# Two transformer blocks on one core: the last output product as a stage of its own, with the roots of its norms on ScalarE and VectorE

## The chip, the cores and the metric

The kernel runs on one core of one Trainium2 chip. The metric is the device time of one execution in microseconds (us), as the median of the runs shown.

## What is computed

The input x has 512 positions of 1024 values in fp32. It goes through two blocks, each applied for two layers. The first block mixes by retention, two convolutions and a gated feed-forward part. The second block mixes by a gated spatial product, by attention and by a linear recurrence. Both end with the same pattern: a merged activation is multiplied by an output matrix, the result is normalised by its root mean square and scaled by a gain, and x is added. The change touches the last time this happens, in the last layer of the second block:

```python
def rmsnorm_2(x, g):
    xf = x.astype(jnp.float32)
    y = xf * lax.rsqrt(jnp.mean(xf * xf, axis=-1, keepdims=True) + EPS)
    return (y * g.astype(jnp.float32)).astype(x.dtype)

def second_block(...):
    for l in range(L):
        ...
        merged = (jax.nn.sigmoid(g_a) * (y_a @ w_proj_a[l])
                  + jax.nn.sigmoid(g_b) * (y_b @ w_proj_b[l])
                  + jax.nn.sigmoid(g_c) * (y_c @ w_proj_c[l]))
        x = x + rmsnorm_2(merged @ w_out[l], post_norm_g[l])
    return x
```

## The kernel before, in words

The program is one long list of instructions, written in the order in which each engine is to run them; nothing reorders it afterwards. Every fp32 product is made as three products of split operands (`mm3`, lines 348 to 350): high times high, high times low, low times high, accumulated in one PSUM bank. Weights come in chunks of 128x1024 through a ring: SyncE (SP) loads them, ScalarE (ACT) makes the high part (line 208), VectorE (DVE) the low part (line 209).

`out_proj` makes the product of a merged activation with an output matrix. The 512 positions are four blocks of 128 rows (`tb`), the 1024 output columns two halves (`hf`), so there are eight PSUM banks in use. The first chunks of the contraction are run through all four blocks; the last four (`tail`) are run block by block, so that one half of one block after the other is finished. With `last=True`, which only the last layer of the second block passes, nothing but the end of the program follows.

What follows each half is the norm. `post_half` takes the sum of squares of a half on ScalarE (line 472, which writes the scaled sum into a column of the small tile `sq`; in the trace it is an ACTIVATE and a read of the accumulator) and multiplies the half by the gain on VectorE (line 478). After the second half VectorE adds the two sums and epsilon (line 476), and GpSimd (POOL) raises the result to the power -0.5 (line 402, `rstd`). `post_norm` then multiplies each half by that root and adds x (line 489, VectorE, two instructions). In the last product the two halves are written to the output straight away (line 564), the first by ScalarE's DMA queue, the second by SP's.

GpSimd has little else to do near the end: its last instructions before these four powers are the two DMA issues that fetch the gain (line 321).

Behind the last instruction of each engine stands the end of the program, which the profile gives to line 1625: each engine has a DRAIN and then takes part in a barrier of all five. SP first waits for all transfers to land. GpSimd collects the arrivals of the others behind its own DRAIN and releases them, clears the semaphores, and a second, like barrier follows.

Of the kernel before, what the change touches and what calls it, by code (L numbers as in the profile page):

```python
# [10 lines left out]
AF = mybir.ActivationFunctionType  # L11
ALU = mybir.AluOpType
# [6 lines left out]
NT = S // 128  # L19
EPS = 1e-6  # L20
# [126 lines left out]
class Stream:  # L147
# [102 lines left out]
    def next(self):  # L250
        return len(self.order) // UNITS
# [9 lines left out]
class Kernel:  # L261
# [202 lines left out]
    def post_half(self, tb, hf, ps, g):  # L464
# [15 lines left out]
        ys.append(y)  # L480
        return r

    def post_norm(self, tb, ps, g):

        r = self.post_half(tb, 1, ps, g)
        _, ys = self.post.pop(tb)
        for hf in range(2):
            x = self.x[tb, hf]
            self.nc.vector.scalar_tensor_tensor(x[:], ys[hf][:], r[:, 0:1], x[:], op0=ALU.mult, op1=ALU.add)
            self.s.f(ys[hf])  # L490

    def out_proj(self, name, l, nk, get, done, g_post, g_pre, spill, last=False, head=4, tail=4):


        ws = self.ws
        gp = [self.bcast(g_post, 512 * hf) for hf in range(2)]
        gn = None if last else [self.bcast(g_pre, 512 * hf) for hf in range(2)]
        ps = {}
        wts = {}

        def w(k):
            if k not in wts:
                wts[k] = [self.ws.take(512, (name, l, 128 * k, (512 * hf, 512))) for hf in range(2)]
            return wts[k]

        def go(k, tb, hfs=(0, 1)):
            op = get(k)
            for hf in hfs:
                if (tb, hf) not in ps:
                    ps[tb, hf] = self.p.t()  # L510
                wh, wl = w(k)[hf]
                t = slice(128 * tb, 128 * tb + 128)
                self.mm3(ps[tb, hf][:], (op.hi[:, t], op.lo[:, t]), (wh, wl), k == 0, k == nk - 1)

        base = ws.floor = ws.next()
        assert head + tail <= nk
        for k in range(head):
            for tb in (0, 1):
                go(k, tb)
            self.tick()  # L520
        for k in range(head):
            for tb in (2, 3):
                go(k, tb)
            done(k)
            ws.floor += 1
            self.tick()
        for k in range(head, nk - tail):
            for tb in range(NT):
                go(k, tb)
            done(k)  # L530
            ws.floor += 1
            self.tick()
        assert ws.floor == base + nk - tail
        for tb in range(NT):
            units = [(k, hf) for hf in range(2) for k in range(nk - tail, nk)]
            if tb == NT - 1 and not last:
                units.sort()
            nk_half = max(n for n, u in enumerate(units) if u[1] == 0)
            pre = ()
            for n, (k, hf) in enumerate(units):  # L540
                go(k, tb, (hf,))
                if n == 1 and not last:
                    if tb >= 2:
                        self.transposes(tb - 2)
                    if tb >= 1:
                        pre = self.pre_norm_parts(tb - 1, gn, spill)
                        next(pre)
                if n == nk_half:
                    if tb == NT - 1:
                        for _ in pre:  # L550
                            pass
                    self.post_half(tb, 0, ps[tb, 0], gp)
                    for _ in pre:
                        pass
                if tb == NT - 1 and hf:
                    done(k)
                    ws.floor += 1
                    if n < 4:
                        ws.ahead(base + nk + AHEAD - 2 + n // 2)
            self.post_norm(tb, ps[tb, 1], gp)  # L560
            if last:
                for hf in range(2):
                    eng = self.nc.sync if hf else self.nc.scalar
                    eng.dma_start(self.out[128 * tb:128 * tb + 128, 512 * hf:512 * hf + 512], self.x[tb, hf][:])
                    self.s.f(self.x.pop((tb, hf)))
        ws.floor = None
        self.s.f(*gp)
        if not last:
            self.pend = self.norm_tail(gn, spill)

    def norm_tail(self, gn, spill):

# [1056 lines left out]
```

## Time and profile before

| what | value |
|---|---|
| median of 3 runs | 3151.83 us (3151.82 to 3152.45) |
| the profiled execution, its own time | 3152.43 us |
| its span in the profile | 3150.7 us |
| granted TensorE clock, mean of the span | 0.999 of full speed |
| PE busy | 3135.4 us (100% of the span) |
| DVE, ACT, POOL busy | 1864.8, 1195.4 and 236.3 us |

The span is what the profiler sees from the first to the last instruction; the execution's own time is 1.73 us longer. The profiled execution is 0.60 us above the median of the runs, and at the upper end of their range. Busy times say which engine has work all the time; what the end of the program waits for is read from the last ten microseconds alone, where PE is already done.

### The profile page before, as it was taken

To read this page: it belongs to the slowest core of one execution; us is meant where nothing else is said; L and a number is where in the kernel's file an instruction comes from. 1 tells how busy PE (TensorE), PEld (TensorE's weight loads), DVE (VectorE), ACT (ScalarE), POOL (GpSimd) and SP (SyncE) were. 2 spreads that over 40 slices of the span, in tenths; PEclk is the share of its full clock that TensorE was granted. 3 is DMA by queue.
4 is the path that set the end of the run, shared out by engine and by line. 5 is a ranking of instruction groups with operands and counts; after the bars stand their busy time and mean duration, and the time that the engine had idled before them with its cause. 6 is when DMAs were issued, how large, how long until landed. Compare 5 with 4: busy or idle time off the path is not lost.

```text
span 3150.7 us, 36918 instructions
## 1 busy us (share of the span) xinstructions
PE 3135.4 (100%) x14814; PEld 2638.9 (84%) x14814; DVE 1864.8 (59%) x2731; ACT 1195.4 (38%) x1801; POOL 236.3 (8%) x365
## 2 busy tenths in 40 slices
PE   9999999999999999999999999999999999999998
PEld 7888888888888888888898888888889888888887
DVE  6687556663568755666458736745546854663643
ACT  4222343343422234333345626622325643642222
POOL 2000010000300010000011001200002000120000
PEclk9999999999999999999999999999999999999999
DMA  6222322232422232223323123332333313433232
GB/s 206 92 90 94 134 86 102 94 120 107 148 107 87 94 134 88 93 101 107 112 95 127 55 99 118 116 140 72 125 124 120 94 67 107 133 114 107 95 106 74
DMA packets 62336, 337.47 MB, mean 107 GB/s; under 512 B 10290, under 2 KB 10418, under 8 KB 27476
## 3 DMA queue, kind: packets, MB, share of 16 engines
q1 hardware_dynamic: 49840, 302.02, 27.4%
q0 software_dynamic: 11312, 31.45, 3.5%
q8 instruction: 117, 1.92, 0.3%
q10 hardware_dynamic: 1012, 1.64, 0.1%
q14 instruction: 55, 0.45, 0.0%
HBM read 310.16 MB, written 8.39 MB: 101 GB/s over the span
## 4 chain that ended last, share of the span: by engine, by line
PE 99%; DMA 0%; ACT 0%; DVE 0%; DVEq 0%; ACTq 0%; issue 0%; POOLq 0%
PE p L348 31%; PE p L350 31%; PE p L349 31%; PE p L452 1%; PE p L691 1%; PE p L1090 1%; PE p L1357 0%; PE p L1063 0%; PE p L1062 0%; PE p L1064 0%; PE p L1061 0%; PE p L1065 0%; DMA s<-in_x_dram 0%; PE p L1234 0%; PE p L990 0%; PE p L678 0%
## 5 line engine op out<-in xcount | busy, mean ns | idle before, releaser
L348 PE MATMUL p<-hh,whi 128*128 128x512 f32 (+1 forms) x2752 | 1048.2, 381 | 0.3 <-ACT hh L455 0.3
L349 PE MATMUL p<-hl,whi 128*128 128x512 f32 (+1 forms) x2752 | 1044.8, 380 | 0.1
L350 PE MATMUL p<-hh,wlo 128*128 128x512 f32 (+1 forms) x2752 | 1044.6, 380 | 0.0
L209 DVE TENSOR_TENSOR wlo<-raw,whi 128x1024 fp32r<-128x1024 f32 x543 | 671.7, 1244 | 470.2 <-ACT whi L208 468.7
L208 ACT ACTIVATE whi<-raw 128x1024 fp32r<-128x1024 f32 x543 | 563.1, 1053 | 320.9 <-PE p L350 193.3
L350 PEld LDWEIGHTS p<-hh,wlo 128*128 128x128 f32 x2752 | 518.5, 188 | 97.8
L348 PEld LDWEIGHTS p<-hh,whi 128*128 128x128 f32 x2752 | 518.7, 188 | 96.6 <-ACT hh L455 0.7
L349 PEld LDWEIGHTS p<-hl,whi 128*128 128x128 f32 x2752 | 518.7, 188 | 96.5 <-DVE hl L459 0.4
L348 PE MATMUL p<-s,whi 128*128 128x512 f32 (+1 forms) x768 | 300.0, 391 | 0.0
L349 PE MATMUL p<-s,whi 128*128 128x512 f32 (+1 forms) x768 | 299.2, 390 | 0.0
L350 PE MATMUL p<-s,wlo 128*128 128x512 f32 (+1 forms) x768 | 299.0, 389 | 0.0
L348 PE MATMUL p<-whi,s 128*128 128x512 f32 x640 | 250.0, 391 | 0.0
L350 PE MATMUL p<-whi,s 128*128 128x512 f32 x640 | 249.1, 389 | 0.0
L349 PE MATMUL p<-wlo,s 128*128 128x512 f32 x640 | 249.0, 389 | 0.0
L332 ACT ACTIVATE s<-s 128x512 fp32r<-128x512 f32 x168 | 103.6, 627 | 362.6 <-DVE s L752 129.4
L726 ACT ACTIVATE s<-p 128x512 f32<-128x512 f32 x96 | 57.3, 597 | 397.7 <-PE p L350 397.7
L876 DVE SCALAR_TENSOR_TENSOR s<-p,pv,s 128x511 f32<-128x511 f32 (+1 forms) x176 | 131.8, 749 | 122.3 <-ACT s L873 119.2
L747 DVE TENSOR_TENSOR s<-p,s 128x512 f32<-128x512 f32 x96 | 66.2, 690 | 195.3 <-PE p L350 195.3
L624 DVE SCALAR_TENSOR_TENSOR s<-s,pv,s 128x511 f32<-128x511 f32 (+14 forms) x240 | 176.0, 733 | 5.7
L350 PEld LDWEIGHTS p<-s,wlo 128*128 128x128 f32 (+1 forms) x768 | 144.2, 188 | 30.5
L349 PEld LDWEIGHTS p<-s,whi 128*128 128x128 f32 (+1 forms) x768 | 144.3, 188 | 29.3
L348 PEld LDWEIGHTS p<-s,whi 128*128 128x128 f32 (+1 forms) x768 | 144.3, 188 | 29.3
(200 smaller groups left out, 3060.0 us busy)
## 6 DMA issues: line engine op xcount, KB each, us to landing
raw<-in_w_dram SPq DMA_DIRECT2D x271, 1024.0 KB, 4.8
s<-in_rows_dram POOLq DMA_DIRECT2D x32, 256.0 KB, 3.8
s<-s POOLq DMA_DIRECT2D x96, 64.0 KB, 2.6
xd<-s SPq DMA_DIRECT2D x24, 256.0 KB, 6.1
s<-xd POOLq DMA_DIRECT2D x24, 256.0 KB, 3.3
s<-s SPq DMA_DIRECT2D x88, 64.0 KB, 2.8
s<-in_cst_dram POOLq DMA_DIRECT2D x16, 256.0 KB, 3.6
s<-in_x_dram POOLq DMA_DIRECT2D x8, 256.0 KB, 5.3
```

The costliest lines, as they stand in the source:

```text
L208: nc.scalar.activation(hi[:], src, AF.Copy)
L209: nc.vector.tensor_tensor(lo[:], src, hi[:].bitcast(F32), op=ALU.subtract)
L332: self.nc.scalar.activation(hi[:, :n], t[:, :n], AF.Copy)
L348: mm(ps, a[0], b[0], start=first, stop=False)
L349: mm(ps, a[0], b[1], start=False, stop=False)
L350: mm(ps, a[1], b[0], start=False, stop=last)
L452: nc.tensor.transpose(ps[:, 128 * q:128 * q + 128], h[:, 128 * q:128 * q + 128], self.ident[:])
L624: nc.vector.scalar_tensor_tensor(c[:, sh:], glu[:, :S - sh], w(k), c[:, sh:], op0=ALU.mult, op1=ALU.add)
L691: mm(po[:, 128 * i:128 * i + 128], st[j][:, 128 * (i - j):128 * (i - j) + 128], v[j][:, 128 * h:128 * h + 128], start=j == 0, stop=j == i)
L726: self.nc.scalar.activation(t[:], pg[:], AF.Sigmoid)
L747: nc.vector.tensor_tensor(sg[:], py[:], sg[:], op=ALU.mult)
L876: nc.vector.scalar_tensor_tensor(t[:, sh:], ps[:, :S - sh], w(k), t[:, sh:], op0=ALU.mult, op1=ALU.add)
```

## The change

The last product leaves `out_proj` for a function of its own, `out_last`, which runs the same products in the same order. Its norm is written in two new functions. The tile of small values has eight columns. Epsilon is added to the first half's sum (line 495) while the second half is still being multiplied. The root is an ACTIVATE with Sqrt on ScalarE, whose input is the second sum and whose bias is the first sum with epsilon (line 502); VectorE takes the reciprocal (line 503). GpSimd has no part in it any more. One Sqrt of a constant, ahead of the stage, brings ScalarE's table in (line 515).

```diff
+    def post_part(self, tb, hf, ps, g):
+        nc, s = self.nc, self.s
+        if hf == 0:
+            self.post[tb] = self.small(8, "sq8"), []
+        sq, ys = self.post[tb]
+        junk, y = s.t(), s.t()
+        nc.scalar.activation(junk[:], ps[:], AF.Square, scale=1.0 / 32.0, accum_out=sq[:, hf:hf + 1])
+        s.f(junk)
+        nc.vector.tensor_tensor(y[:], ps[:], g[hf][:], op=ALU.mult)
+        self.p.f(ps)
+        if hf == 0:
+            nc.vector.tensor_scalar(sq[:, 2:3], sq[:, 0:1], EPS, None, op0=ALU.add)
+        ys.append(y)
+
+    def post_last(self, tb):
+        nc, s = self.nc, self.s
+        sq, ys = self.post.pop(tb)
+        nc.scalar.activation(sq[:, 3:4], sq[:, 1:2], AF.Sqrt, bias=sq[:, 2:3])
+        nc.vector.reciprocal(sq[:, 4:5], sq[:, 3:4])
+        for hf, y in enumerate(ys):
+            x = self.x.pop((tb, hf))
+            nc.vector.scalar_tensor_tensor(x[:], y[:], sq[:, 4:5], x[:], op0=ALU.mult, op1=ALU.add)
+            eng = nc.sync if hf else nc.scalar
+            eng.dma_start(self.out[128 * tb:128 * tb + 128, 512 * hf:512 * hf + 512], x[:])
+            s.f(y, x)
+
+    def out_last(self, go, ps, gp, nk, tail, done):
+        nc = self.nc
+        warm = self.small(1, "warm")
+        nc.scalar.activation(warm[:], self.half[:, 0:1], AF.Sqrt, scale=-1.0)
+        for tb in range(NT):
+            for hf in range(2):
+                for k in range(nk - tail, nk):
+                    go(k, tb, (hf,))
+                self.post_part(tb, hf, ps[tb, hf], gp)
+            self.post_last(tb)
+        for k in range(nk - tail, nk):
+            done(k)
+        self.ws.floor = None
+        self.s.f(*gp)
...
         assert ws.floor == base + nk - tail
+        if last:
+            self.out_last(go, ps, gp, nk, tail, done)
+            return
         for tb in range(NT):
             units = [(k, hf) for hf in range(2) for k in range(nk - tail, nk)]
-            if tb == NT - 1 and not last:
+            if tb == NT - 1:
                 units.sort()
...
             self.post_norm(tb, ps[tb, 1], gp)
-            if last:
-                for hf in range(2):
-                    eng = self.nc.sync if hf else self.nc.scalar
-                    eng.dma_start(self.out[128 * tb:128 * tb + 128, 512 * hf:512 * hf + 512], self.x[tb, hf][:])
-                    self.s.f(self.x.pop((tb, hf)))
         ws.floor = None
         self.s.f(*gp)
-        if not last:
-            self.pend = self.norm_tail(gn, spill)
+        self.pend = self.norm_tail(gn, spill)
```

The order of PE's and SP's instructions is the same in both programs. Three engines differ, all in this last stage. In the rows below, `whi` and `raw` are weight chunks, `p` is a PSUM bank, `s` a tile of 128x512, and `[waits ...]` names the engines and queues whose semaphores the instruction waits for.

ScalarE, from the last weight chunks to the end of the first block's norm, before:

```order
L208 ACTIVATE whi_23600<-raw_23527 128x1024 [waits DMAHW3_49,PE_49,Activation_49]
L208 ACTIVATE whi_23680<-raw_23527 128x1024 [waits PE_49,Activation_49]
L472 ACTIVATE s_1526_23697,sq<-p_888_23564 128x512 [waits PE_49]
L472 ACTIVATE s_1528_23713,sq<-p_889_23572 128x512 [waits PE_49]
L564 DMA out_dram<-s_1492_23000 128x512 [waits DVE_49]
```

and with the change:

```order
L208 ACTIVATE whi_23600<-raw_23527 128x1024 [waits DMAHW3_49,PE_49,Activation_49]
L515 ACT_TABLE_LOAD
L515 ACTIVATE warm<-half 128x1
L208 ACTIVATE whi_23682<-raw_23527 128x1024 [waits PE_49,Activation_49]
L490 ACTIVATE s_1526_23699,sq_23698<-p_888_23564 128x512 [waits PE_49]
L490 ACTIVATE s_1528_23716,sq_23698<-p_889_23572 128x512 [waits PE_49]
L502 ACTIVATE sq_23698<-sq_23698 128x1 [waits DVE_49,Activation_49]
L508 DMA out_dram<-s_1492_23000 128x512 [waits DVE_49]
```

One table load and one Sqrt of a constant stand between the last two weight chunks, and each block's root stands behind its second Square, ahead of its DMA issue. This is the only table load from there to the end.

VectorE, the last block to the end of the program, before:

```order
L478 TENSOR_TENSOR s_1539_23818<-p_894_23636,s_1524_23560 128x512 [waits Activation_49]
L476 SCALAR_TENSOR_TENSOR sq<-sq 128x1 [waits Activation_49]
L478 TENSOR_TENSOR s_1541_23834<-p_895_23640,s_1525_23562 128x512
L489 SCALAR_TENSOR_TENSOR s_1498_23012<-s_1539_23818,rstd,s_1498_23012 128x512 [waits DMASW5_49,Pool_49]
L489 SCALAR_TENSOR_TENSOR s_1499_23014<-s_1541_23834,rstd,s_1499_23014 128x512 [waits DMASW6_49,DVE_49]
L1625 UNCONDITIONAL_BRANCH
```

and with the change:

```order
L492 TENSOR_TENSOR s_1539_23820<-p_894_23636,s_1524_23560 128x512 [waits Activation_49]
L495 TENSOR_SCALAR sq_23818<-sq_23818 128x1
L492 TENSOR_TENSOR s_1541_23837<-p_895_23640,s_1525_23562 128x512 [waits Activation_49]
L503 RECIPROCAL sq_23818<-sq_23818 128x1 [waits Activation_49]
L506 SCALAR_TENSOR_TENSOR s_1498_23012<-s_1539_23820,sq_23818,s_1498_23012 128x512 [waits DMASW5_49,DVE_49]
L506 SCALAR_TENSOR_TENSOR s_1499_23014<-s_1541_23837,sq_23818,s_1499_23014 128x512 [waits DMASW6_49]
L1666 UNCONDITIONAL_BRANCH
```

The small sum ahead of the second multiplication is gone; a small addition stands behind the first multiplication, and the reciprocal stands behind the second.

GpSimd, from the last loads of x and of the gain to the end of the program, before:

```order
L409 DMA s_1499_23014<-xd 128x512 [waits DMASW6_49,DVE_49]
L321 DMA s_1524_23560<-in_rows_dram 128x512 [waits DMASW7_49,DVE_49,PE_49]
L321 DMA s_1525_23562<-in_rows_dram 128x512 [waits DMASW0_49,DVE_49]
L402 TENSOR_TENSOR rstd<-sq,half 128x1 [waits DVE_49] x2
L402 TENSOR_TENSOR rstd<-sq,half 128x1 [waits DVE_49,Pool_49] x2
L1625 UNCONDITIONAL_BRANCH
L1625 ISA [waits barrier_Pool_Activation_PE_DVE_SP_gather]
```

and with the change:

```order
L409 DMA s_1499_23014<-xd 128x512 [waits DMASW6_49,DVE_49]
L321 DMA s_1524_23560<-in_rows_dram 128x512 [waits DMASW7_49,DVE_49,PE_49]
L321 DMA s_1525_23562<-in_rows_dram 128x512 [waits DMASW0_49,DVE_49]
L1666 UNCONDITIONAL_BRANCH
L1666 ISA [waits barrier_Pool_Activation_PE_DVE_SP_gather]
```

The four powers are gone, so GpSimd's branch to the end of the program, with its DRAIN, stands right behind the second load of the gain.

## Rows read from the trace of the kernel before

**Rows 1.** The page: span, and the chain that ended last by engine.
```profile
span 3150.7 us, 36918 instructions
...
PE 99%; DMA 0%; ACT 0%; DVE 0%; DVEq 0%; ACTq 0%; issue 0%; POOLq 0%
```

**Rows 2.** The chain of waits from 3139.5 us: start us, us, what.
```profile
3140.11 0.24 PE p L350
...
3141.37 0.59 POOLq L1625
...
3141.98 0.04 DVE s L489
```

**Rows 3.** The timeline of the last block: start, us, engine, line, operation [idle before].
```profile
3140.37 0.60 ACT L472 ACTIVATE s<-p 128x512 f32<-128x512 f32 x1 [1.92 <-PE p L350]
3140.86 0.20 ACT L472 ACTIVATION_READ_ACCUMULATOR s<-p 128x1 f32 x1
...
3141.09 0.16 DVE L476 SCALAR_TENSOR_TENSOR sq<-sq 128x1 f32<-128x1 f32 x1 [1.92 <-ACT s L472]
3141.17 0.68 DVE L478 TENSOR_TENSOR s<-p,s 128x512 f32<-128x512 f32 x1
3141.39 0.55 POOL L402 TENSOR_TENSOR rstd<-sq,half 128x1 f32<-128x1 f32 x1 [4.89 <-DVE sq L476]
3141.98 1.41 DVE L489 SCALAR_TENSOR_TENSOR s<-s,rstd,s 128x512 f32<-128x512 f32 x2
...
3143.42 0.33 SPq L564 DMA_DIRECT2D out_dram<-s  x1
```

**Rows 4.** Line 1625, the program's end: queue, operation, ns min/median/max, first to last start.
```profile
L1625 PEldq DRAIN  x1: 4267/4267/4267, 3136.1 to 3136.1; - x1
...
L1625 SPq DRAIN  x2: 7/7/7, 3145.9 to 3145.9; - x2
L1625 POOLq DRAIN  x1: 8502/8502/8502, 3141.4 to 3141.4; - x1
L1625 DVEq DRAIN  x1: 1349/1349/1349, 3142.1 to 3142.1; - x1
...
L1625 POOLq EVENT_SEMAPHORE  x2: 17/17/17, 3149.9 to 3150.0; - x2
```

**Rows 5.** The waits of SP's own queue from 3110 us: total, times, longest us.
```profile
SPq L1625 <- PEq L1625: 4.6, 2, 4.1
```

**Rows 6.** The timeline of GpSimd before the four powers.
```profile
3072.75 0.54 POOL L321 DMA_DIRECT2D s<-in_rows_dram  x1 [0.60 <-DVE s L333]
```

**Rows 7.** The timeline of ScalarE around the last weight chunk and the first Squares.
```profile
3099.79 1.99 ACT L208 ACTIVATE whi<-raw 128x1024 fp32r<-128x1024 f32 x2
3110.51 1.06 ACT L208 ACTIVATE whi<-raw 128x1024 fp32r<-128x1024 f32 x1 [8.73 <-PE p L350]
...
3124.05 0.60 ACT L472 ACTIVATE s<-p 128x512 f32<-128x512 f32 x1 [2.03 <-PE p L350]
```

**Rows 8.** ScalarE's groups by form: count | busy us, mean ns | idle before.
```profile
L1187 ACT ACTIVATE s<-p,pv 128x512 f32<-128x512 f32 x20 | 15.4, 770 | 5.9 <-PE p L350 5.9
...
L1257 ACT ACT_TABLE_LOAD x4 | 5.1, 1283 | 0.1
...
L1450 ACT ACTIVATE warm<-half 128x1 f32<-128x1 f32 x1 | 0.2, 203 | 0.0
```

**Rows 9.** VectorE's groups of small operations: count | busy us, mean ns | idle before.
```profile
L429 DVE SCALAR_TENSOR_TENSOR sq<-sq 128x1 f32<-128x1 f32 x22 | 8.5, 387 | 4.0 <-ACT s L426 4.0
...
L1077 DVE RECIPROCAL asm<-asm 128x4 f32<-128x4 f32 x16 | 2.9, 178 | 9.4 <-ACT s L1069 9.4
...
L1342 DVE TENSOR_SCALAR gmv<-gmv 128x1 f32<-128x1 f32 x8 | 1.2, 154 | 0.3
```

**Rows 10.** The timeline of VectorE: a dependent instruction right behind its producer.
```profile
3096.85 0.69 DVE L747 TENSOR_TENSOR s<-p,s 128x512 f32<-128x512 f32 x1 [1.15 <-PE p L350]
3097.58 0.69 DVE L752 TENSOR_TENSOR s<-s,s 128x512 f32<-128x512 f32 x1
```

More of the change, by code (lines that the diff above doesn't have):

```diff
@@ L541, in out_proj @@
                 go(k, tb, (hf,))
-                if n == 1 and not last:
+                if n == 1:
                     if tb >= 2:
```

## The prediction

> **What bounds the kernel now.** The page comes first: of a span of 3150.7 us the chain that ended last is TensorE for 99% [rows 1]. The order of PE's instructions is the same in both programs, so the body stays, and only the stretch behind the last product can change. The chain of waits shows it: the last product ends at 3140.11 + 0.24 = 3140.35, and the last piece that carries work begins at 3141.98 with GpSimd just ahead of it [rows 2]. In the timeline of the last block the reader is to see two roads from the accumulator's end (3140.86 + 0.20 = 3141.06). One is the small sum on VectorE at 3141.09, then GpSimd's power, 3141.39 to 3141.94. The other is the second multiplication on VectorE, 3141.17 to 3141.85. The two final operations start at 3141.98, the second store is issued at 3143.42 [rows 3].
>
> The chain ends with that work at about 3143.4, but the span lasts to 3150.7. So the view to read is line 1625, the end of the program. SP has seen all transfers land and finished its drains at 3145.9. VectorE's drain ends at 3142.1 + 1.35 = 3143.4, PE's at 3136.1 + 4.27 = 3140.4. GpSimd's DRAIN starts at 3141.4, right behind its last power was issued, and runs 8.50 us, to 3149.9; GpSimd's part of the barrier comes at 3149.9 to 3150.0, directly after it [rows 4]. So the barrier waits 4.0 us (3149.9 - 3145.9) for GpSimd alone, and 0.8 us later the span ends. SP's own waits put 4.1 us down to PE [rows 5]; that is the releaser inferred from the barrier's semaphore, and PE's drain had ended 5.5 us before SP's.
>
> **The change part by part.**
>
> *The four powers go.* GpSimd's last work is then the second load of the gain, issued at 3072.75 + 0.54 = 3073.3 [rows 6]. Its DRAIN comes right behind. At the price of the row, 8.50 us, it ends at 3081.8, which is 64 us before SP is ready. The cover is the 72.6 us from there to 3145.9. Late next is SP, which waits for the last store to land, so the barrier starts at 3145.9 and the span ends 0.8 us later. That is worth 4.0 us. The bounds: 0, if the drain ends where it did for another reason; 4.0 at most, since SP is the next to arrive. I take 4.0, because the only row of a GpSimd drain behind work starts with that engine's own last instruction and not with anything else's end.
>
> The Trainium skill, "VectorE: DVE Perf Modes", section "The DRAIN you can't avoid", says that the DRAINs at the beginning and end of a program are some 12 ns on all five engines. By that page this term would be nothing and the sum -0.03 us. SP's drains of 7 ns agree with it; GpSimd's of 8502 ns doesn't, and the measurement decides.
>
> *The chain behind the last product.* Before, the final operations wait for the later of multiplication (3141.85) and power (3141.94), and start at 3141.98. Now the second multiplication starts where the small sum did, 3141.09, and ends at 3141.09 + 0.68 = 3141.77. ScalarE's root starts at 3141.06. No row shows a Sqrt of one column with a bias; a one-column ACTIVATE took 0.203 us, and an ACTIVATE of 512 columns with pointer operands took 770 ns where the Square without took 600 [rows 3, 8], so 0.20 to 0.37 us, that is 3141.43 at the latest. It is hidden behind the multiplication, and costs nothing unless it takes over 0.7 us. The reciprocal stands behind the multiplication. The nearest row is 178 ns for four columns [rows 9]. It starts between 3141.69 (the small sum was overlapped by 0.08 us by what followed it, 3141.09 + 0.16 against 3141.17 [rows 3]) and 3141.77, and ends between 3141.87 and 3141.95. A dependent VectorE operation started 0.04 us behind its producer's end (3096.85 + 0.69 against 3097.58 [rows 10]). So the final operations start between 3141.91 and 3141.99: -0.07 to +0.01 us. The upper bound of a small operation is the 387 ns group beside GpSimd's work [rows 9], which would make it +0.2 us. I take the middle of the near rows, -0.03 us: the reciprocal's row is the nearest in operation and size.
>
> *The addition of epsilon* (154 ns by rows 9) follows the first multiplication, in VectorE's idle 1.92 us before the last block's small sum [rows 3]: nothing; without that cover, 0.15 us. *The roots of the first three blocks* lie in ScalarE's like idle time, 1.92 to 2.03 us before a Square [rows 3, 7]: nothing. Each stands ahead of its block's store, which waits for VectorE anyway.
>
> *The table load and the warm Sqrt* stand on ScalarE behind a weight chunk that ends at 3099.79 + 1.99 = 3101.78; the next chunk starts at 3110.51, after 8.73 us of waiting for PE [rows 7]. A load takes 1283 ns, the warm Sqrt 203 ns [rows 8]: 1.49 us inside 8.73. Without the cover the last chunk would be split 1.49 us later, which would still be some ten microseconds ahead of the products that end before the Square at 3124.05 [rows 7]: nothing either way.
>
> *PE, SP, the stores:* same instructions in the same order, and both stores follow the final operations at the same distance.
>
> **The sum.** -4.0 - 0.03 = -4.0 us, of the profiled execution's own time: 3152.43 - 4.0 = 3148.4. It is 0.60 us above the median of the runs, so against the median 3151.83 - 4.0 = **3147.8 us**, 0.13% less. A difference of under 0.2% (6.3 us) is about what a measurement of this kernel can't tell from no change.
>
> **The rivals.**
>
> *The drain doesn't hold the end of a timed run* (8%): the 8.5 us are no cost of the power, or the change removes them only on paper. For it speaks that GpSimd's spans are rough and that there is one such row only. Against it: the barrier's instructions on GpSimd start at the drain's end, and nothing else is late. Then only the chain moves: 3151.83 - 0.03 = 3151.8 us. The 12 ns that the Trainium skill's page gives, above, would come out here.
>
> *The drain follows the stores, slower* (4%): GpSimd's drain ends 4.0 us behind the landing because it waits for the landed data, whatever GpSimd did last. Then the end follows the final operations alone, and these start later than now, with the reciprocal behind the multiplication at its upper bound: +0.2 us, 3152.0 us. It decides as soon as the final operations start later than 1.63 us after the last product's end (3141.98 - 3140.35). Against it: the drain starts at 3141.4, 4 us before anything landed, and no row ties the two.
>
> *ScalarE switches tables in each block* (3%): Square and Sqrt don't share a table, and a load stands between them. Then the last root ends at 3141.06 + 1.28 + 0.37 = 3142.71, the reciprocal at 3142.93, and the final operations start at 3142.97, 0.99 us later: 3148.8 us with the drain gone. Against it: the order of ScalarE has one load in this stage, ahead of the stage.
>
> The Trainium skill, "ScalarE: Activation LUTs", section "Table sets: the hidden batching unit", gives a rule against this change: functions of different sets shouldn't be mixed, and each switch costs about 2.7 us with its drain. By that price this rival would come to some 3150.2 us, as an estimate. The rows have 1283 ns for the load; no run so far shows the drain behind it.
>
> **How the numbers follow.** The forecast has 85%, the rivals 8, 4 and 3%. The forecast's own range is the sum against the two ends of the runs, 3147.8 and 3152.45 - 4.0 = 3148.4, with 0.07 us less and 0.2 us more for the chain, and half the 0.6 us between the runs on the lower side: 3147.4 to 3148.6. The times at the program's end are read to 0.1 us, several of them in one sum, which adds 0.4 us below; the third rival ends the range above: 3147.0 to 3149.0. The first two rivals, 12%, are left out. All cases lie within 6.3 us of the median, so within 0.2% has 96%; 2% on either side are for something that no row shows.
>
> **What would show it.** Right: in line 1625's rows GpSimd's long DRAIN starts near 3073, the barrier starts within 0.1 us of SP's drains, and the span is 3146.7 us. The root ends before the second multiplication; the final operations start 1.56 to 1.64 us behind the last product; the stage has one table load, inside the idle 8.7 us. Wrong: a drain on GpSimd that still ends near 3149.9, a table load between Square and Sqrt, a reciprocal that waits for ScalarE, or a PE that ends at another time than 3140.4.

## The result, and the profile after

The change makes the kernel slower: 3171.61 us (3171.37 to 3171.82, 4 runs) against 3152.14 us for the kernel before in the same comparison (3151.82 to 3152.46), a ratio of 1.0062 with a 95% interval of 1.0050 to 1.0073. The forecast was 3147.8 us. In the spans the difference is 3169.8 - 3150.7 = 19.1 us.

The page and the end of the chain of waits of the changed kernel (start us, us, what):

```profile
span 3169.8 us, 36923 instructions
...
PE 3157.4 (100%) x14814; PEld 2637.0 (83%) x14814; DVE 1866.6 (59%) x2735; ACT 1198.2 (38%) x1807; POOL 233.9 (7%) x361
```

```profile
3163.32 0.24 PE p L350
...
3164.31 0.36 DVE s L492
...
3165.10 0.75 DVE s L506
```

The last product ends at 3163.32 + 0.24 = 3163.56. Before it ended at 3140.35 [rows 2]: PE is done 23.2 us later, with the same 14814 matmuls. From there to the end of the span it is 3169.8 - 3163.56 = 6.2 us, and was 3150.7 - 3140.35 = 10.35. So two things happened: the stretch that the prediction was about became 4.1 us shorter, and the body, of which it said that it stays, became 23.2 us longer.

The end of the program, line 1666 now (queue, operation, count, ns min/median/max, first to last start), to be compared with [rows 4]:

```profile
L1666 POOLq DRAIN  x1: 8469/8469/8469, 3094.2 to 3094.2; - x1
...
L1666 SPq DRAIN  x3: 7/7/7, 3169.0 to 3169.3; - x3
...
L1666 POOLq EVENT_SEMAPHORE  x2: 17/17/17, 3169.0 to 3169.1; - x2
```

GpSimd's long DRAIN runs from 3094.2, where PE still has 69 us to go, and the barrier starts with SP's drain at 3169.0.

The timeline of the new stage on ScalarE and VectorE, to be compared with [rows 3, 7]:

```profile
3123.74 1.28 ACT L515 ACT_TABLE_LOAD   x1
3125.03 0.20 ACT L515 ACTIVATE warm<-half 128x1 f32<-128x1 f32 x1
3132.85 1.06 ACT L208 ACTIVATE whi<-raw 128x1024 fp32r<-128x1024 f32 x1 [7.61 <-PE p L350]
...
3163.59 0.60 ACT L490 ACTIVATE s<-p 128x512 f32<-128x512 f32 x1 [2.11 <-PE p L350]
3164.08 0.20 ACT L490 ACTIVATION_READ_ACCUMULATOR s<-p 128x1 f32 x1
3164.31 0.29 ACT L502 ACTIVATE sq<-sq 128x1 f32<-128x1 f32 x1
```

```profile
3164.31 0.69 DVE L492 TENSOR_TENSOR s<-p,s 128x512 f32<-128x512 f32 x1 [2.04 <-ACT s L490]
3164.91 0.15 DVE L503 RECIPROCAL sq<-sq 128x1 f32<-128x1 f32 x1
3165.10 1.41 DVE L506 SCALAR_TENSOR_TENSOR s<-s,sq,s 128x512 f32<-128x512 f32 x2
```

The root takes 0.29 us and is hidden behind the multiplication; the final operations start 3165.10 - 3163.56 = 1.54 us behind the last product, 0.09 us sooner than before.

Where the 23.2 us went is read from PE's groups by form (line, operation, moving operand, stationary operand, count | busy us, mean ns). First before, then with the change:

```profile
L348 PE MATMUL p<-hh,whi 128*128 128x512 f32 x2496 | 974.2, 390 | 0.0
L350 PE MATMUL p<-hh,wlo 128*128 128x512 f32 x2496 | 971.5, 389 | 0.0
L349 PE MATMUL p<-hl,whi 128*128 128x512 f32 x2496 | 971.4, 389 | 0.0
L348 PE MATMUL p<-s,whi 128*128 128x512 f32 x752 | 293.7, 391 | 0.0
L349 PE MATMUL p<-s,whi 128*128 128x512 f32 x752 | 292.8, 389 | 0.0
L350 PE MATMUL p<-s,wlo 128*128 128x512 f32 x752 | 292.8, 389 | 0.0
L348 PE MATMUL p<-whi,s 128*128 128x512 f32 x640 | 250.0, 391 | 0.0
L350 PE MATMUL p<-whi,s 128*128 128x512 f32 x640 | 249.1, 389 | 0.0
L349 PE MATMUL p<-wlo,s 128*128 128x512 f32 x640 | 249.0, 389 | 0.0
```

```profile
L348 PE MATMUL p<-hh,whi 128*128 128x512 f32 x2496 | 974.8, 391 | 0.0
L349 PE MATMUL p<-hl,whi 128*128 128x512 f32 x2496 | 972.3, 390 | 0.0
L350 PE MATMUL p<-hh,wlo 128*128 128x512 f32 x2496 | 971.9, 389 | 0.0
L348 PE MATMUL p<-s,whi 128*128 128x512 f32 x752 | 297.3, 395 | 0.0
L349 PE MATMUL p<-s,whi 128*128 128x512 f32 x752 | 296.6, 394 | 0.0
L350 PE MATMUL p<-s,wlo 128*128 128x512 f32 x752 | 296.4, 394 | 0.0
L348 PE MATMUL p<-whi,s 128*128 128x512 f32 x640 | 253.1, 396 | 0.0
L349 PE MATMUL p<-wlo,s 128*128 128x512 f32 x640 | 252.6, 395 | 0.0
L350 PE MATMUL p<-whi,s 128*128 128x512 f32 x640 | 250.8, 392 | 0.0
```

The six groups that read a 128x512 tile of activations (`s`), as moving or as stationary operand, are busy 1646.8 us in sum and were 1627.4, so 19.4 us more. The three groups that read the normalised activation (`hh`, `hl`) rose by 1.9 us in 2917. These durations overlap, since each product starts some 227 ns behind the one before: they show which products grew, and not yet what PE lost. The starts in the two traces show that. From its start to the next product's start, a product of weights with `s` took 227.1 ns before and 232.1 ns with the change; over some 4200 of them that is 21.2 us. The products of weights with `hh` or `hl` lost 2.2 us, and all others are 0.2 us shorter: 23.2 us in sum.

No idle time stands before any of these groups, and the granted clock is 1.00 of full speed (2.4 GHz, the upper of its two levels) in each stretch of 500 us up to 3000, with the change and in e1 below. In each such stretch the products with `s` lose 1.2 us or more. So the matmuls with `s` themselves became longer, all through the program, also in layers that the change doesn't touch. Traffic beside PE is not the cause: of these products, those that ran while VectorE, ScalarE and GpSimd had no operation and no DMA packet was on its way rose as much, from 226.7 ns (455 of them) to 232.1 ns (473).

What those matmuls share with the change is the memory layout, which the built program gives. `sq8` is a new size of small tile, with six buffers of eight fp32 columns, 192 bytes per partition. The small tiles lie ahead of the 48 tiles `s`, so all of these moved by 192 bytes: the first from byte 129760 of each partition to 129952. The weights (`whi`, `wlo`) and `hh`, `hl` lie ahead of them and stayed. Counted within 256 bytes (the address modulo 256), all operands of the three-part products (lines 348 to 350) started at byte 224 before; now `s` starts at 160. The kernel before has a tile in this pool, `shift` (line 269), that nothing reads or writes; its 96 bytes bring `s` to 224.

### The profile page after: what moved, and what is told of

It is laid out like the page before. It is cut to its first block, busy times and chain, and to the rows that moved or that the text cites. A ratio compares the mean times of both kernels' runs of the same rounds, so it can differ in the third digit from the quotient of the medians.

```text
span 3169.8 us, 36923 instructions
## 1 busy us (share of the span) xinstructions
PE 3157.4 (100%) x14814; PEld 2637.0 (83%) x14814; DVE 1866.6 (59%) x2735; ACT 1198.2 (38%) x1807; POOL 233.9 (7%) x361
## 4 chain that ended last, share of the span: by engine, by line
PE 99%; DMA 0%; DVE 0%; ACT 0%; issue 0%; DVEq 0%; POOL 0%; ACTq 0%
PE p L349 31%; PE p L348 31%; PE p L350 31%; PE p L452 1%; PE p L732 1%; PE p L1131 1%; PE p L1398 0%; PE p L1105 0%; PE p L1104 0%; PE p L1102 0%; PE p L1103 0%; PE p L1106 0%; PE p L1275 0%; PE p L1031 0%; PE p L719 0%; PE p L720 0%
## 5 line engine op out<-in xcount | busy, mean ns | idle before, releaser
L348 PE MATMUL p<-hh,whi 128*128 128x512 f32 (+1 forms) x2752 | 1048.0, 381 | 0.3 <-ACT hh L455 0.3
L348 PEld LDWEIGHTS p<-hh,whi 128*128 128x128 f32 x2752 | 517.7, 188 | 98.1 <-ACT hh L455 0.7
L348 PE MATMUL p<-s,whi 128*128 128x512 f32 (+1 forms) x768 | 303.7, 395 | 0.0
L349 PE MATMUL p<-s,whi 128*128 128x512 f32 (+1 forms) x768 | 302.8, 394 | 0.0
L348 PE MATMUL p<-whi,s 128*128 128x512 f32 x640 | 253.1, 396 | 0.0
L348 PEld LDWEIGHTS p<-s,whi 128*128 128x128 f32 (+1 forms) x768 | 143.9, 187 | 33.8
```

The lines of the kernel that those rows point to most:

```text
L348: mm(ps, a[0], b[0], start=first, stop=False)
L349: mm(ps, a[0], b[1], start=False, stop=False)
```

## The experiments

Theory A: the layout slows PE, and the stage itself does what was forecast. Rival B: the new stage slows PE. The first four kernels tell these apart, and settle the drain. Besides the two kernels compared, only e1 was run more than once; each other time below is that of one run, and the runs of one kernel lie up to 1.6 us apart (the kernel before, 13 runs).

**e1_no_new_tile.** The change, without the new size of tile:

```diff
-            self.post[tb] = self.small(8, "sq8"), []
+            self.post[tb] = self.small(4, "sq"), []
...
-        nc.vector.reciprocal(sq[:, 4:5], sq[:, 3:4])
+        r = self.small(1, "rstd")
+        nc.vector.reciprocal(r[:, 0:1], sq[:, 3:4])
...
-            nc.vector.scalar_tensor_tensor(x[:], y[:], sq[:, 4:5], x[:], op0=ALU.mult, op1=ALU.add)
+            nc.vector.scalar_tensor_tensor(x[:], y[:], r[:, 0:1], x[:], op0=ALU.mult, op1=ALU.add)
```

> The change with no new kind of small tile: the sums and the root stay in a tile of four columns, the reciprocal goes into a small tile of one column that the kernel before has too. All 48 tiles of 128x512 then lie where they lay before the change. Theory A (the change slows PE because the eight-column tile moves every 128x512 tile by 192 bytes): PE is as before, its last product ends within 0.3 us of 3140.4, the matmuls that read such a tile have a mean near 390 ns again; the drain on GpSimd still starts near 3073, so 3147.8 us, 0.6 us either way. Rival B (the new stage itself, its instructions or their number, slows PE): PE ends near 3163.6 and the time is near 3171.6 us.

Measured: 3148.10 us (3147.16 to 3148.55, 10 runs) against 3152.34 us before (13 runs), a ratio of 0.9986, interval 0.9977 to 0.9996. The end of its program:

```profile
L1667 POOLq DRAIN  x3: 46/93/8467, 3071.5 to 3145.1; - x3
L1667 SPq DRAIN  x3: 7/7/7, 3144.6 to 3144.9; - x3
L1667 PEldq DRAIN  x2: 13/2140/4267, 3134.9 to 3144.9; - x2
```

PE's busy time is 3134.5 us, and the group L348 with `s` moving is at 391 ns again. PE ended at 3134.9 + 4.27 = 3139.2, 0.9 us ahead of what was expected at the earliest; the runs of this kernel spread over 1.4 us, so nothing is read from that. Rival B falls. For this kernel the forecast's 3147.8 us is 0.3 us off, and the gain over the kernel before is 4.2 us where 4.0 were forecast.

**e2_before_pad192.** The kernel before, with `shift` made 192 bytes wider:

```diff
-        self.sm.tile([128, 24], F32, tag="shift", name="shift", bufs=1)
+        self.sm.tile([128, 24 + 48], F32, tag="shift", name="shift", bufs=1)
```

> The kernel before, unchanged but for 192 bytes more per partition in a small tile that nothing reads or writes. Theory A: the matmuls with such tiles slow down as they do in the change, PE ends 23 us later, the time is 3152 + 23 = 3175 us, more than with the change because the drain on GpSimd stays. Rival B: 3152 us, as before.

Measured: 3175.51 us, 23.2 us more than before, with no instruction added, left out or moved in the order. Its group L348 with `s` moving has the 297.3 us and 395 ns of the change.

**e3_after_pad256.** The change, with `shift` 64 bytes wider (`24 + 16`), so that `s` is 256 bytes behind its place before.

> The change with 64 bytes more in the tile that nothing uses, so that the 128x512 tiles lie 256 bytes behind their place before, not 192. Theory A with the place counted within 256 bytes (or a part of it): PE as before, 3147.8 us. Theory A with the distance itself or a larger period: near 3171 us. Rival B: near 3171 us.

Measured: 3148.51 us. The distance is larger than in the change, and the cost is gone: the place within 256 bytes counts, or within a part of it.

**e4_with_power.** As e1, with a power on GpSimd at its old place:

```diff
+        self.rstd(sq[:, 3:4], 1)
         r = self.small(1, "rstd")
         nc.vector.reciprocal(r[:, 0:1], sq[:, 3:4])
```

> As e1_no_new_tile, and GpSimd again raises a small value to a power in each block, at the place where it did before (now of the root; its result is read by nothing). Theory on the drain: GpSimd's DRAIN starts near 3141.4 again, runs 8.5 us, and holds the end at about 3150.7 of span: 3151.8 us, 4.0 us more than e1_no_new_tile. Rival (the 4 us come from the shorter chain behind the last product, or from elsewhere): the time of e1_no_new_tile.

Measured: 3152.42 us, as the kernel before (3152.34 us). The end of its program:

```profile
L1668 POOLq EVENT_SEMAPHORE  x4: 17/17/17, 3149.8 to 3150.5; - x4
L1668 POOLq DRAIN  x3: 46/93/8502, 3141.3 to 3150.3; - x3
L1668 SPq DRAIN  x3: 7/7/7, 3145.5 to 3150.0; - x3
```

Nothing reads this power's result, and VectorE's chain is that of e1: in both the final operations start 1.5 us behind the last product. The 4.3 us are GpSimd's drain alone: it starts at 3141.3, and the barrier starts at its end, 3149.8, 4.3 us behind SP's first drain.

**Where in 256 bytes.** Four kernels move `s` from its place in e1 by a wider `shift` (`24 + 16`, `+ 32`, `+ 8` and `+ 24` columns), with the weights and the normalised activation at 224.

> As e1_no_new_tile, with the 128x512 tiles moved by 64 bytes, so that they start 32 bytes behind a multiple of 256 (e1: 224, the change: 160). Theory P128 (the place within 128 bytes decides; 96 is fast, 32 is slow): as with the change, PE 23 us later, 3171 us. Theory P256 (the place within 256 decides): slow or fast, since 32 was not seen yet.

> As e1_no_new_tile, moved by 128 bytes, to 96 behind a multiple of 256. Theory P128: the place within 128 bytes is that of e1, so 3148 us. Theory P256: another place, slow, some 3171 us.

> As e1_no_new_tile, moved by 32 bytes, to a multiple of 256. If what counts is where a row of a tile starts, a full multiple should be at least as fast as e1: 3148 us or less. If what counts is that all of PE's operands start at the same place (the weights and the normalised activation stay at 224): 3171 us.

> As e1_no_new_tile, moved by 96 bytes, to 64 behind a multiple of 128 and of 256. Where a row starts counts in steps of 64: as e5_pad32. All operands must start at one place: 3171 us.

Measured, with the difference to e1:

| kernel | `s` starts at, in 256 bytes | time, us | more than e1, us |
|---|---|---|---|
| e1_no_new_tile, e3_after_pad256 | 224 | 3148.10, 3148.51 | 0, 0.4 |
| e5_pad64 | 32 | 3170.57 | 22.5 |
| the change | 160 | 3171.61 | 23.5 |
| e5_pad128 | 96 | 3174.09 | 26.0 |
| e5_pad32 | 0 | 3177.40 | 29.3 |
| e6_pad96 | 64 | 3180.78 | 32.7 |

Every place but 224 is slow. The place within 128 bytes doesn't decide: 96 and 224 are the same in 128, and differ by 26 us. A full multiple of 256 is among the worst. The two cheapest of the slow places differ by 1.0 us, less than the runs of one kernel do, so these times don't tell which of the two is cheaper. All this is what is expected if what counts is not where a row starts but whether all operands start at the same place; it could still be that 224 is a good place by itself.

**The same place, or a good place.** Three more kernels put an unused tile further ahead. e8 has it behind `hl`, ahead of the weight ring, so that weights and `s` move together; e9 and e10 have it at the very front, so that all operands move. Of e9 (e10 has 8 columns, e8 the same line as e9 behind the two tiles):

```diff
+        fixed.tile([128, 48], F32, tag="gap", name="gap")
         self.ident = fixed.tile([128, 128], F32, tag="ident", name="ident")
```

> As e1_no_new_tile, but with 192 unused bytes ahead of the weight ring, so that the weights and the 128x512 tiles both start at 160 in 256, and only the normalised activation stays at 224. Theory S (PE's operands must start at the same place in 256 bytes): the products of weights with the tiles are fast again, near 227 ns apart, the products of weights with the normalised activation, 7488 of them, are slow: 6 ns more each, some 45 us, near 3193 us. Theory O (each operand's own place counts, 224 is the good one): both are slow, 3171 us plus the same 45 or more, near 3215 us or above.

> As e1_no_new_tile, with everything that PE reads for its products moved by 192 bytes: all operands at 160 in 256. Theory S: as fast as e1_no_new_tile, 3148 us. Theory O: every product is slow, 3215 us or above.

> As e9, moved by 32 bytes: all operands at a multiple of 256. Theory S: 3148 us, as e1_no_new_tile. Theory O: slow, as e9 or worse, since the tiles alone at this place cost 29 us.

Measured: e9 3147.65 us and e10 3148.74 us, both as e1. All operands at 160, the place that costs 23.5 us for `s` alone, cost nothing; nor do all at 0. Theory O falls: what counts is that the operands of a product start at the same place in 256 bytes.

e8 took 3173.72 us, 25.6 us more than e1. The groups show that the slow products changed sides:

```profile
L349 PE MATMUL p<-hh,whi 128*128 128x512 f32 x2496 | 985.2, 395 | 0.0
L351 PE MATMUL p<-hh,wlo 128*128 128x512 f32 x2496 | 978.4, 392 | 0.0
L350 PE MATMUL p<-hl,whi 128*128 128x512 f32 x2496 | 974.3, 390 | 0.0
L349 PE MATMUL p<-s,whi 128*128 128x512 f32 x752 | 295.7, 393 | 0.0
L351 PE MATMUL p<-s,wlo 128*128 128x512 f32 x752 | 294.1, 391 | 0.0
L350 PE MATMUL p<-s,whi 128*128 128x512 f32 x752 | 293.0, 390 | 0.0
L349 PE MATMUL p<-whi,s 128*128 128x512 f32 x640 | 250.2, 391 | 0.0
L351 PE MATMUL p<-whi,s 128*128 128x512 f32 x640 | 249.2, 389 | 0.0
L350 PE MATMUL p<-wlo,s 128*128 128x512 f32 x640 | 249.0, 389 | 0.0
```

Weights with `hh`, `hl` rose by 20.8 us over the kernel before, weights with `s` by 3.8 where they rose by 19.4 in the change. The size was missed: 45 us were expected, at 6 ns for each of 7488 products, and 2.8 ns each came, where the 4176 products with `s` in the change paid 4.6 ns. The expectation took its price from the wrong direction: in the change the activation lies 64 bytes ahead of the weights within 256 (160 against 224), in e8 64 bytes behind them (224 against 160). The kernel with the direction of e8 is e5_pad64, where `s` lies 64 bytes behind the weights (224 + 64 is 32, counted within 256):

```profile
L348 PE MATMUL p<-s,whi 128*128 128x512 f32 x752 | 296.5, 394 | 0.0
L350 PE MATMUL p<-s,wlo 128*128 128x512 f32 x752 | 295.3, 393 | 0.0
L349 PE MATMUL p<-s,whi 128*128 128x512 f32 x752 | 293.3, 390 | 0.0
L348 PE MATMUL p<-whi,s 128*128 128x512 f32 x640 | 253.7, 396 | 0.0
```

In the order shown, the means with `s` moving are those of e8 with `hh`, `hl` moving, within 1 ns (394, 393, 390 against 395, 392, 390), and 2.6 ns more in the mean than before. With the activation as the stationary operand the price is higher: 5.8 ns in the three groups of e5_pad64, and in e8 6 ns (75.9 against 74.7 us in a group of 192 with `hh` stationary). In the change it was 4.9 ns with `s` moving and 4.4 ns with `s` stationary. So the price depends on the direction of the distance and on which operand is the moving one.

**e11_with_product.** As e4, with a multiplication in place of the power:

```diff
-        self.rstd(sq[:, 3:4], 1)
+        w = self.small(1, "rstd")
+        nc.gpsimd.tensor_tensor(w[:, 0:1], sq[:, 3:4], self.half[:, 0:1], op=ALU.mult)
```

> As e4_with_power, but GpSimd multiplies the root by a constant instead of raising it to a power. If the long drain belongs to whatever GpSimd runs last: 3152.3 us, the drain starts near 3141.4 and takes 8.5 us. If it belongs to the power: the drain is short, and the time is that of e1_no_new_tile, 3148.1 us.

Measured: 3152.37 us, as with the power:

```profile
L1669 POOLq DRAIN  x3: 46/93/8142, 3141.7 to 3150.3; - x3
L1669 SPq DRAIN  x3: 7/7/7, 3145.9 to 3150.1; - x3
```

The drain is 8.1 us behind a multiplication, 8.5 behind a power, and 8.5 behind the DMA issue of e1. It belongs to the end of the program on GpSimd, and not to the power.

## Why the prediction was wrong

The step that failed stands in its first paragraph: "The order of PE's instructions is the same in both programs, so the body stays", repeated under "PE, SP, the stores". The order is the same; the addresses aren't. The new size of small tile moved the operands `s` by 192 bytes, and PE took 23.2 us more for the same products. e1 and e2 show it from both sides: the change without the move is fast, the move without the change is slow. No rival had it, and the range, whose widest case was 0.99 us on the path behind the last product, could not hold it; 2% on either side were left for what no row shows. One of the prediction's signs of being wrong did name what came: "a PE that ends at another time than 3140.4". What could have raised the question was at hand: the change's description says that the tile of small values "has eight columns", and the kernel before has a tile `shift` that nothing uses, whose only effect is the layout.

Point by point, the rest held:

- *The four powers go*, 4.0 us: GpSimd's drain started at 3094.2 and the barrier with SP's drain. The stretch behind the last product became 4.1 us shorter; e4 against e1 gives 4.3 us. The rival in which the drain doesn't hold the end and the slower rival, in which it follows the stores, both fall: it ended at 3102.7, 66 us before the barrier started. The Trainium skill's 12 ns ("VectorE: DVE Perf Modes", "The DRAIN you can't avoid") are near SP's 7 ns, and not near GpSimd's DRAIN at the end, which is 8142 to 8502 ns in each profile of this case, nor near PE's 4267 ns [rows 4].
- *The chain behind the last product*, -0.07 to +0.01 us, taken as -0.03: it was -0.09 us (1.54 against 1.63). The root took 0.29 us, inside the 0.20 to 0.37; the reciprocal 0.15 where 0.178 was taken, and it overlapped the multiplication by 0.09 us, which puts the sum at the low end of what was forecast, 0.02 us below it.
- *The table load*: one, of 1.28 us, with the warm Sqrt right behind it, inside ScalarE's wait for PE, which still lasts 7.61 us behind the warm Sqrt. No second load; that rival falls. The drain of 1.38 us that the Trainium skill ("ScalarE: Activation LUTs", "What ACT_TABLE_LOAD costs") has behind a load isn't to be seen here: the warm Sqrt starts at 3125.03, and 3123.74 + 1.28 is 3125.02.
- *The addition, the roots of the first three blocks, the stores*: off the path, as forecast.
- *What a measurement can tell*: the prediction put 0.2% (6.3 us) as what can't be told from no change. That was too coarse: the 4.2 us of e1 are told by ten and thirteen runs, whose ranges don't meet (3148.55 at most against 3151.66 at least).

The version that beats both kernels is e1: the change with the small values in kinds of tiles that were there already.

## What to carry to other kernels

A change that adds or widens a tile may move every tile behind it, as `sq8` moved 48 here. Before saying that untouched work stays as it is, compare where its operands lie, not only the order of its instructions. Where PE bounds a kernel with fp32 products like these, try the operands of a product at the same place in 256 bytes, and look at the mean of its groups by form: 391 against 395 ns, in one group of 752, was the trace of 23 us.

GpSimd's last instruction before the end of the program sets when its long DRAIN starts. Here an operation of 0.55 us on GpSimd in the last block cost 4 us, because a DRAIN of 8.5 us stood behind it.

## What the runs showed of the hardware that was not expected

The time of PE's fp32 products depends on where their operands lie relative to each other. When the tiles `s` alone lie elsewhere within 256 bytes, already at a distance of 32, it is 22.5 to 32.7 us here, of 3148; a distance of 256 costs nothing (0.4 us, within the runs' spread), and neither does moving all operands together (e9 and e10, 0.5 us less and 0.6 us more than e1). It holds with `s` as the moving operand (11.0 us more in the three groups of the change) and as the stationary one (8.4 us more).

Some things stay open. Why the price differs with the distance (64 bytes either way is the cheapest, 22.5 and 23.5 us; the others cost 26.0 to 32.7), with its direction and with the role of the operand wasn't tried. Nor was it found out what the 3.8 us are that the products with `s` still paid in e8, nearly all of them (3.5 us) with `s` moving. Nor was it tried whether the moving operand clashes with the stationary operand of its own product or with that of the next one, which is loaded meanwhile.

GpSimd's DRAIN at the end of the program took 8.1 to 8.5 us behind each of the three that stood before it: a power, a multiplication, or the issue of a DMA. What it waits for was not found out.
